# Hybrid pooling and SSD layer on one core: work of the mixing stage moved between VectorE and GpSimd, with other buffers and another order of loads at its start

## The chip, the cores and the metric

The kernel runs on one NeuronCore of one Trainium2 chip. The metric is the device time of one execution in microseconds (us), the median of the runs made; a lower time is better. In the views, PE is TensorE, PEld its weight loads, DVE is VectorE, ACT is ScalarE, POOL is GpSimd and SP is the engine whose queue issues nearly all DMAs.

## The reference, cut to what matters

One decoder layer works on 1024 prompt tokens and on 8 samples of 8 tokens each. Two gated feed-forward blocks enclose the token mixing, and the mixing is where the change lies:

```python
proj = hn @ w_in                       # u, z, x/B/C, dt, two gates
branch_pool = pool_mix(u) @ pool_w_out
xbc = silu(causal_conv(xbc))           # x: 32 heads of 64; B, C: 4 groups of 128
# SSD over chunks of 128 tokens, per head:
a_cs = cumsum(dt * A)                  # within the chunk
y    = ((C @ B.T) * exp(a_cs[l] - a_cs[s])) @ (dt * x)   # inside the chunk, causal
y   += exp(a_cs) * (C @ h_prev)                          # from the state
st   = B.T @ (exp(a_cs[-1] - a_cs) * dt * x)             # the chunk's state
h    = exp(a_cs[-1]) * h_prev + st
y    = y + d_skip * x
yg   = y * silu(z); yg = yg * rsqrt(mean(yg**2 over the group) + eps) * ssd_norm
merged = sigmoid(gate0) * branch_pool + sigmoid(gate1) * (yg @ ssd_w_out)
x = x + merged @ w_o
```

## The kernel before, in words

The tokens are worked on in two halves: half 0 has 512 prompt tokens, half 1 the other 512 and the 64 sample tokens (576 columns). Channels lie on the 128 partitions. Every f32 product of the large matrices is made of three fp32r products: ACT rounds an operand to a high part (L355 for activations, L294 for weights), DVE subtracts to get the low part (L357 or L359, L295), and PE adds three matmuls into one PSUM bank.

The program opens three stages, each with a pool of SBUF memory of its own: first feed-forward block and input projection, mixing, and second feed-forward block. A pool's memory is given to the next stage's tiles, so the first write into such a tile waits until the tile that lay there has been read for the last time. Two sets of buffers lie outside the stages: `act` (42 tiles) and `pair` (8 tiles). In the first stage `fx` takes from the stage's own pool (17 tiles).

In mixing, PE's main thread runs `pool_branch` for both halves (matmuls `pgm`, then `pbp`), then for each half `ssd_out` and `merge` (`pso`) and `out_proj` (`pwo`). Beside it runs the chain `scan`, which goes through eight groups of heads, (half, group) from (0,0) to (1,3). Chains are generators: the main thread calls `tick()` between blocks of matmuls, and a chain is continued when the estimated PE time that it asked for has gone by. The framework then orders each engine's queue by priority and an estimate of its own. Each engine works its queue strictly in order.

For a group, `fetch` loads B, C (`bc`) and x (`xs`, four blocks of channels). `ssd_a` for a chunk of 128 tokens loads `ab`, the cumulated a of the group's eight heads, to all partitions; PE turns x (`pxT`) and makes C·B (`pcb`); DVE makes `xdt` (x·dt, L1338) and `xd` (x·dt·decay, L1347), both from PSUM; ACT makes `ea` (L1355) and the decays (L1357, L1358), DVE multiplies them by the masked C·B (L1359); GpSimd scales x by d_skip (L1349). `ssd_st` makes the state with one matmul group `pst`, which needs `xd`. `ssd_b` makes `pyo` (from the state) and `pyd` (from `ab` and `xdt`), and adds them. In half 1 a fifth chunk has the samples: eight units, each of which loads a state `h`, scales and updates it (L1403) and stores it (L1405). `z` is loaded with chunk 3 of every group (L1470).

When a group is through, `gating` starts as a chain: y·z (L1495), the norm by `rstd` (squares on ACT, sums `ssq` on DVE L380, one matmul group `pss`, then `prb`), y·norm on DVE (L1504), and the split into `yhl` for the `pso` matmuls. `merge` combines the branches: a side chain `head` makes (1+gate)·acc on DVE (L1594) and adds the pooling branch on GpSimd (L1595) ahead of the last `pso` of each block; behind it two DVE steps (L1608, L1609) and the split into `mh`, `ml` remain.

Of the kernel before, what the change touches and what calls it, by code (L numbers as in the profile page):

```python
# [44 lines left out]
STEP_S = 1.0  # L45
POST, RIPE = 1.0, 3.0
GP = (1.5, 1.2)
# [14 lines left out]
def tile_hybrid_pool_ssd_macaron(  # L62
# [189 lines left out]
    acs_d = [dp.tile([4, NH, CH], F32, tag=f"acsd{h}", name=f"acsd{h}") for h in HALVES]  # L252
# [116 lines left out]
    def rstd(tiles, h, count, out, pace=1.0):  # L369

        N = NTOK[h]
        nch = 4 + h
        s = act((P, N), name="ssq")
        for i, x in enumerate(tiles):
            if i == 0:
                S.activation(s, x, AF.Square)
            else:
                q = act((P, N), name="sq")
                S.activation(q, x, AF.Square)
                V.tensor_tensor(s, s, q, op=ALU.add)  # L380
# [20 lines left out]
        S.copy(r[:, :512], pr)  # L401
# [425 lines left out]
    def mix_dt(h, xs):  # L827
# [9 lines left out]
        def chain():  # L837
# [43 lines left out]
            dma(acs_d[h].rearrange("c h l -> (c h) l"), afm)  # L881
            V.tensor_tensor(dtd, dtd, dt[:, :128], op=ALU.mult)
# [172 lines left out]
    def proj_pair(kind, ia, ib, xs):  # L1055
# [22 lines left out]
        def after(p, i, bk):  # L1078
# [3 lines left out]
            if p == "1":  # L1082
                out[i] = {"a": fx(name="ra"), "b": fx(name="rb")}
# [216 lines left out]
    def ssd_a(h, g, c, Bf, Cf, xs4, dts, h0s):  # L1300
# [11 lines left out]
        for q in range(nq):  # L1312
            ab = act((P, hq, L), name="ab")
            if smp:
                dma(ab, acs_sd[g * HPG : (g + 1) * HPG].partition_broadcast(P))
            else:
                r0 = g * HPG + q * hq
                dma(ab, acs_d[h][c, r0 : r0 + hq].partition_broadcast(P))
# [26 lines left out]
        else:  # L1345
            xd = act((P, 512), name="xd")
            V.tensor_tensor(xd[:L, :].rearrange("p (h d) -> p h d", d=HD), px[:L, :].rearrange("p (h d) -> p h d", d=HD),  # L1347
# [3 lines left out]
        for q, ab in enumerate(abs_):  # L1351
            av = ab.rearrange("p (q h) l -> p q h l", h=2)
            ev = ea[:, q * (hq // 2) : (q + 1) * (hq // 2), :]
            for hh in range(2):
                S.activation(ev[hh * HD : (hh + 1) * HD], av[hh * HD : (hh + 1) * HD, :, hh, :], AF.Exp)  # L1355
            for i in range(hq):
                S.activation(ab[:L, i, :], ab[:L, i, :], AF.Relu, bias=acs[:L, hc + q * hq + i : hc + q * hq + i + 1], scale=-1.0)  # L1357
            S.activation(ab[:L], ab[:L], AF.Exp, scale=-1.0)  # L1358
            V.tensor_tensor(ab[:L], ab[:L], cbm[:L, :L].unsqueeze(1).broadcast_to([L, hq, L]), op=ALU.mult)  # L1359
# [10 lines left out]
    def ssd_b(h, g, c, a, hold, Cf, y4, dts, h0s):  # L1370
# [8 lines left out]
        if smp:  # L1379
# [12 lines left out]
            for i, (pr, bh) in enumerate(units):  # L1392
# [12 lines left out]
                dma(dst, h0)  # L1405
                if pr == 3:
# [19 lines left out]
        for i in range(HPG):  # L1426
            m_ = abs_[i // abs_[0].shape[1]][:L, i % abs_[0].shape[1], :]
# [31 lines left out]

    def ssd_group(h, g, Bf, Cf, xs4, dts, zs):  # L1460
# [3 lines left out]
        for c in range(4 + h):  # L1464
            ga = ssd_a(h, g, c, Bf, Cf, xs4, dts, h0s)
            next(ga)
            if c == 3:
                for j in range(4):
                    z = act((P, NTOK[h]), name="z")
                    dma(z, zd[h][g * 4 + j])  # L1470
                    zs.append(z)
# [5 lines left out]
            if prev:  # L1477
                yield from ssd_b(h, g, *prev, Cf, y4, dts, h0s)
            prev = (c, a)
        yield step  # L1480
        yield from ssd_b(h, g, *prev, ssd_st(h, g, *prev, dts), Cf, y4, dts, h0s)
# [9 lines left out]
    def gating(h, g, y4, zs, out):  # L1491

        N = NTOK[h]
        for j in range(4):
            (G if j % 2 and (h, g) != (1, NG - 1) else V).tensor_tensor(y4[:, j, :N], y4[:, j, :N], zs[j], op=ALU.mult)  # L1495
            yield GP[0]
        rr = []
        yield from rstd([y4[:, j, :N] for j in range(4)], h, 512, rr, GP[0])
# [3 lines left out]
        for j in range(4):  # L1502
            a, b, _ = pair(N, "yhl")
            V.tensor_tensor(y4[:, j, :N], y4[:, j, :N], rr[0], op=ALU.mult)  # L1504
# [50 lines left out]
    cs = start(scan())  # L1555

# [25 lines left out]
    def merge(h, gs, acc):  # L1582
# [4 lines left out]

        def head():
# [9 lines left out]
        ch = start(head(), MP)  # L1598
        yn = ynorm(h, gs)
        mh, ml = [], []  # L1600
        for m in range(KD):
            pb = dense(ssd_w_out[0], gs[0] * 4, 4 * len(gs), m * P, [yn], name="pso")[0]
            while merged[0] <= m:
                ch.step()
            a_, b_ = act((P, N), F32R, "mh"), act((P, N), F32R, "ml")
            with tc.high_priority(HP_EV):
                for pt, (a, b) in zip(pb, PIECES[h]):
                    V.scalar_tensor_tensor(t1[m][:, a:b], t1[m][:, a:b], 1.0, pt[:, : b - a], op0=ALU.add, op1=ALU.mult)  # L1608
            V.tensor_tensor(t1[m], t1[m], acc[m], op=ALU.add)  # L1609
# [168 lines left out]
```

## Time and profile before

| | |
|---|---|
| median of 3 runs | 2937.12 us (2936.72 to 2939.24) |
| the profiled execution's own time | 2939.05 us |
| its span, first to last instruction | 2937.3 us |
| PE busy | 2828.8 us, 96% of the span |
| DVE, ACT, POOL busy | 1784.7, 1385.2 and 993.0 us |
| mixing stage | from about 1523 us (first `pgm`) to 2177 us (end of `pwo`) |

The profiled execution's time is its span and 1.75 us around it; it lies 1.93 us above the median. PE is busy nearly all the time, so a change can bring only what PE waits, what it runs at less than its full clock, and what it loses between instructions. These waits stand mostly between 1520 and 2060 us.

### The profile page before, as it was taken

What the parts mean: (1) busy time and instruction counts of PE and PEld (TensorE: products, weight loads), DVE (VectorE), ACT (ScalarE), POOL (GpSimd) and SP (SyncE); (2) the same over time, 40 slices, a digit from 0 to 9 for tenths busy, and PEclk for the clock granted to TensorE, in tenths of its full rate; (3) what the DMA queues carried; (4) which work ended last, traced back from release to release, by engine and by line L of the source; (5) the groups of instructions that cost most, each with busy time, mean ns of one, the idle gap of its engine ahead of it and who ended that gap; (6) DMA issues with size and microseconds to landing.
All of it is one profiled execution on the core that took longest, in us unless ns stands there. A gap on an engine that the chain in (4) does not pass through costs nothing.

```text
span 2937.3 us, 51029 instructions
## 1 busy us (share of the span) xinstructions
PE 2828.8 (96%) x18494; PEld 2570.2 (88%) x18494; DVE 1784.7 (61%) x2843; ACT 1385.2 (47%) x3024; POOL 993.0 (34%) x1011
## 2 busy tenths in 40 slices
PE   7999999999999999999989999898999999999998
PEld 6999999789989989898977887677999999987898
DVE  6655555434484687887976877766665544453422
ACT  5444444323354555564556766566233444442422
POOL 6434444000133455454422332323234444440000
PEclk9999999999999999999999999999999999999999
DMA  4575554856445555543367777786774532236652
GB/s 134 166 224 182 160 172 132 277 188 194 112 126 163 159 179 159 183 127 124 98 221 240 235 235 232 229 271 184 237 241 153 161 98 77 81 101 212 218 156 72
DMA packets 530332, 507.97 MB, mean 173 GB/s; under 512 B 36884, under 2 KB 374664, under 8 KB 530072
## 3 DMA queue, kind: packets, MB, share of 16 engines
q1 hardware_dynamic: 530064, 504.72, 54.0%
q8 instruction: 145, 2.38, 0.3%
q14 instruction: 107, 0.88, 0.1%
q10 hardware_dynamic: 16, 0.00, 0.0%
HBM read 361.77 MB, written 143.05 MB: 172 GB/s over the span
## 4 chain that ended last, share of the span: by engine, by line
PE 44%; DVE 6%; ACT 3%; DMA 3%; issue 1%; POOL 1%; SPq 1%; POOLq 0%; ACTq 0%; DVEq 0%
PE pw L163 19%; PE po L163 9%; PE pso L163 4%; PE pwo L163 3%; PE pbp L163 3%; PE pg L163 1%; PE pu L163 1%; ACT ab L1357 1%; PE pyd L163 1%; DVE wl L444 1%; DVE ct L940 1%; PE pst L163 1%; DMA wraw<-in_ffn_w_in_dram 0%; DVE xs L1504 0%; DVE ab L1359 0%
## 5 line engine op out<-in xcount | busy, mean ns | idle before, releaser
L163 PE MATMUL pw<-X,wh 128*128 128x288 f32 (+1 forms) x2484 | 624.0, 330 | 11.9 <-ACT t L1120 5.3
L163 PE MATMUL pw<-X,wl 128*128 128x288 f32 (+1 forms) x1644 | 472.9, 288 | 0.8 <-DVE wl L444 0.8
L163 PEld LDWEIGHTS pw<-X,wh 128*128 128x128 f32 x2484 | 417.7, 188 | 51.5 <-ACT t L1120 6.7
L163 PE MATMUL pw<-hl,wh 128*128 128x512 f32 x1072 | 390.5, 398 | 3.1 <-DVE t L1129 2.1
L444 DVE TENSOR_TENSOR wl<-s,wh 128x512 fp32r<-128x512 f32 x288 | 223.3, 776 | 200.6 <-ACT wh L443 179.1
L163 PE MATMUL pw<-hi,wh 128*128 128x288 f32 x1120 | 332.1, 297 | 1.3 <-ACT t L596 1.3
L163 PE MATMUL pw<-lo,wh 128*128 128x288 f32 x1120 | 329.7, 294 | 0.0
L163 PE MATMUL pw<-hi,wl 128*128 128x288 f32 x1120 | 329.6, 294 | 0.0
L295 DVE TENSOR_TENSOR wl<-wraw,wh 128x512 fp32r<-128x512 f32 x228 | 164.2, 721 | 249.2 <-ACT wh L294 236.9
L163 PEld LDWEIGHTS pw<-X,wl 128*128 128x128 f32 x1644 | 310.6, 189 | 1.9 <-DVE wl L444 1.8
L437 POOL TENSOR_TENSOR s<-wraw,wraw 128x512 f32<-128x512 f32 x144 | 196.0, 1361 | 333.7 <-DVE wl L444 216.7
L163 PE MATMUL pw<-hl,wl 128*128 128x256 f32 x1072 | 299.6, 280 | 0.2 <-DVE wl L444 0.2
L294 ACT ACTIVATE wh<-wraw 128x512 fp32r<-128x512 f32 x228 | 137.8, 606 | 326.0 <-PE po L163 229.1
L444 DVE TENSOR_TENSOR wl<-wraw,wh 128x512 fp32r<-128x512 f32 x216 | 177.0, 819 | 123.0 <-ACT wh L443 116.3
L443 ACT ACTIVATE wh<-s 128x512 fp32r<-128x512 f32 x288 | 180.8, 629 | 146.4 <-PE pw L163 139.1
L163 PEld LDWEIGHTS pw<-hl,wh 128*128 128x128 f32 x1072 | 201.9, 188 | 40.6 <-DVE t L1129 2.9
L163 PEld LDWEIGHTS pw<-hi,wh 128*128 128x128 f32 x1120 | 210.1, 188 | 12.6 <-ACT t L596 1.8
L163 PE MATMUL po<-hh,wh 128*128 128x288 f32 (+1 forms) x800 | 211.0, 324 | 3.6 <-ACT hh L355 3.4
L163 PE MATMUL po<-hh,wl 128*128 128x288 f32 (+1 forms) x800 | 210.9, 322 | 0.5 <-DMA wl<-part 0.5
L163 PE MATMUL po<-hr,wh 128*128 128x288 f32 (+1 forms) x800 | 210.9, 323 | 0.0
L163 PEld LDWEIGHTS pw<-lo,wh 128*128 128x128 f32 x1120 | 210.2, 188 | 0.0
L163 PEld LDWEIGHTS pw<-hi,wl 128*128 128x128 f32 x1120 | 210.1, 188 | 0.0
(384 smaller groups left out, 6340.7 us busy)
## 6 DMA issues: line engine op xcount, KB each, us to landing
wraw<-in_ffn_w_in_dram SPq DMA_DIRECT2D x188, 256.0 KB
wh<-part SPq DMA_DIRECT2D x156, 256.0 KB
wl<-part SPq DMA_DIRECT2D x156, 256.0 KB
wraw<-in_w_in_dram SPq DMA_DIRECT2D x144, 256.0 KB
wraw<-in_ffn_w_out_dram SPq DMA_DIRECT2D x120, 256.0 KB
part<-ph SPq DMA_DIRECT2D x80, 256.0 KB
part<-pr SPq DMA_DIRECT2D x80, 256.0 KB
ab<-acsd SPq DMA_DIRECT2D x64, 256.0 KB
```

What stands on the lines that cost most here:

```text
L163: T.matmul(out, lhsT, rhs, start=start, stop=stop, skip_group_check=free)
L294: S.activation(wh, raw, AF.Copy)
L295: V.tensor_tensor(wl, raw, wh.bitcast(F32), op=ALU.subtract)
L437: G.tensor_tensor(t, a, b, op=op)
L443: S.activation(wh, a, AF.Copy)
L444: V.tensor_tensor(wl, a, wh.bitcast(F32), op=ALU.subtract)
L940: V.scalar_tensor_tensor(o, f(j), w[j], o, op0=ALU.mult, op1=ALU.add)
L1357: S.activation(ab[:L, i, :], ab[:L, i, :], AF.Relu, bias=acs[:L, hc + q * hq + i : hc + q * hq + i + 1], scale=-1.0)
```

## The change

It has six parts, all in mixing or at its start.

1. `xd` is made by GpSimd from `xdt` (in SBUF) instead of by DVE from PSUM; for that the decay `dtd` is no longer multiplied by dt beforehand.
2. `gating` multiplies y by the norm factor on GpSimd, except for the last group (1,3), pauses 1.5 of estimated PE time behind each such step, and `rstd` waits 2.5 longer there before its matmuls `pss` are queued.
3. `merge` of half 0 works in another order: acc + pso first, then (1+gate) times it, both on DVE, and the pooling branch is added last, by GpSimd. There is no `head` chain; the loads run two blocks ahead.
4. Heads of a group are held as even and odd ones: `ab`'s first tile has heads 0, 2, 4, 6, its second 1, 3, 5, 7. Each tile takes one ACT step for `ea` instead of two of half the length. The table `acs_d` in DRAM is written in that order, by eight DMAs per half instead of one; the samples' `ab` comes by two DMAs of 256-byte rows instead of one of 2 KB rows.
5. In half 1 `z` is loaded within the samples' units (after unit 4's state is stored), not with chunk 3.
6. The last gate blocks of the input projection take `ra` and `rb` from `act`, not from the stage's pool, and `scan` is started one step ahead, so that its first loads are recorded ahead of `pool_branch`.

```diff
-        yield 2.0 * max(pace, 0.75)
+        yield wait + 2.0 * max(pace, 0.75)
...
-            dma(acs_d[h].rearrange("c h l -> (c h) l"), afm)
-            V.tensor_tensor(dtd, dtd, dt[:, :128], op=ALU.mult)
+            for i in range(HPG):
+                dma(acs_d[h][:, :, i % 2, i // 2, :].rearrange("c g l -> (c g) l"), afm[i::HPG])
...
-                out[i] = {"a": fx(name="ra"), "b": fx(name="rb")}
+                new = act if len(xs) == 1 else fx
+                out[i] = {"a": new(name="ra"), "b": new(name="rb")}
...
-            V.tensor_tensor(xd[:L, :]..., px[:L, :]..., dtd..., op=ALU.mult)
+            G.tensor_tensor(xd[:L, :]..., xp[:L, :]..., dtd..., op=ALU.mult)
...
+                if i == Z_UNIT:
+                    load_z(h, g, zs)
...
-            if c == 3:
+            if c == 3 and h == 0:
...
-            V.tensor_tensor(y4[:, j, :N], y4[:, j, :N], rr[0], op=ALU.mult)
+            (V if last else G).tensor_tensor(y4[:, j, :N], y4[:, j, :N], rr[0], op=ALU.mult)
+            if not last:
+                yield GP[0]
...
     cs = start(scan())
+    cs.step()
...
+                    if h == 0:
+                        V.tensor_tensor(acc[m][:, a:b], acc[m][:, a:b], pt[:, : b - a], op=ALU.add)
...
+            if h == 0:
+                V.scalar_tensor_tensor(t1[m], t1[m], 1.0, acc[m], op0=ALU.add, op1=ALU.mult)
+                G.tensor_tensor(t1[m], t1[m], acs[m], op=ALU.add)
+            else:
+                V.tensor_tensor(t1[m], t1[m], acc[m], op=ALU.add)
```

Three places show how the queues change. The first is SP's queue where mixing begins: `gd` is the store of the last gate blocks, `dts`, `bc` and `xs` are the first loads of `scan`, `wraw` are weights. Before:

```order
L916 DMA gd_4_220<-ra_17602 128x576
L291 DMA wraw_18055<-in_pool_w_out_dram 128x4x128
L916 DMA gd_5_221<-rb_17603 128x576
L1318 DMA ab_17773<-acsd_115 128x512
L1318 DMA ab_17775<-acsd_115 128x512
L291 DMA wraw_18073<-in_pool_w_out_dram 128x4x128
L1526 DMA dts_17753<-dtp_272 128x576
L1518 DMA bc_17755<-cv_16_136 128x512
L1519 DMA bc_17756<-cv_20_140 128x512
L1521 DMA xs_3234_17757<-cv_0_120 128x512
```

And in the changed kernel:

```order
L291 DMA wraw_17931<-in_pool_w_out_dram 128x4x128
L1534 DMA dts_17748<-dtp_272 128x576
L1526 DMA bc_17750<-cv_16_136 128x512
L1527 DMA bc_17751<-cv_20_140 128x512
L1529 DMA xs_3228_17752<-cv_0_120 128x512
L1529 DMA xs_3228_17752<-cv_1_121 128x512
L1529 DMA xs_3228_17752<-cv_2_122 128x512
L916 DMA gd_4_220<-ra_17614 128x576
L1529 DMA xs_3228_17752<-cv_3_123 128x512
L1526 DMA bc_17759<-cv_17_137 128x512
L916 DMA gd_5_221<-rb_17615 128x576
```

`dts` and the x of the first group now stand ahead of the two gate stores, not behind them, and five loads of `pool_w_out` weights that stood ahead of `dts` follow later. In the built program `dts` waits for the two `gd` stores before the change, and for the four `zd` stores (which stand ahead of both pieces) after it.

The second is PE's queue where the norm of group (0,3) is made (`pss` needs `ssq`, the sum of squares). Before:

```order
L163 MATMUL pso_20505<-yhl_19401,wh_20506 128x512 x2
L163 MATMUL pso_20505<-yhl_19401,wl_20508 128x512
L163 MATMUL pso_20505<-yhl_19430,wh_20506 128x512
L163 MATMUL pss_20496<-ones,ssq_20398 128x1 x4
L163 MATMUL pso_20505<-yhl_19430,wh_20506 128x512
L163 MATMUL pso_20505<-yhl_19430,wl_20508 128x512
L163 MATMUL pyo_20516<-bc_19684,hst_20361 128x128 x4
L163 MATMUL pyd_20521<-ab_20323,xdt_20376 64x128 x4
L163 MATMUL pyd_20521<-ab_20325,xdt_20376 64x128 x4
```

And in the changed kernel, from the same block of `pso` on:

```order
L163 MATMUL pso_20471<-yhl_19563,wh_20472 128x512 x2
L163 MATMUL pso_20471<-yhl_19563,wl_20474 128x512
L163 MATMUL pyo_20485<-bc_19672,hst_20337 128x128 x4
L163 MATMUL pyd_20490<-ab_20293,xdt_20352 64x128
L163 MATMUL pyd_20490<-ab_20295,xdt_20352 64x128
L163 MATMUL pyd_20490<-ab_20293,xdt_20352 64x128
L163 MATMUL pyd_20490<-ab_20295,xdt_20352 64x128
L163 MATMUL pyd_20490<-ab_20293,xdt_20352 64x128
L163 MATMUL pyd_20490<-ab_20295,xdt_20352 64x128
L163 MATMUL pyd_20490<-ab_20293,xdt_20352 64x128
L163 MATMUL pyd_20490<-ab_20295,xdt_20352 64x128
L163 MATMUL pss_20506<-ones,ssq_20372 128x1 x4
```

`pss` moved behind the rest of that block, `pyo` and `pyd`; `pyd` now takes its two `ab` tiles in turn.

The third is GpSimd's queue in the merge of half 0: `acc` or `t` with `ac` is the addition of the pooling branch, `xs` with `r` the norm factor, `xd` the state's scaled x, `hst` the old state's decay, `xs` with `ea` the sum of y. Before, around the fifth to seventh addition:

```order
L1454 TENSOR_TENSOR hst_21417<-hst_21288,dts_18337 128x512
L1595 TENSOR_TENSOR acc_3736_20089<-acc_3736_20089,ac_21402 128x512
L1437 TENSOR_TENSOR xs_3770_20240<-xs_3770_20240,ea_21308 128x4x128
L1595 TENSOR_TENSOR acc_3749_20147<-acc_3749_20147,ac_21457 128x512
L1349 TENSOR_TENSOR xs_3770_20240<-xs_3770_20240,Dcol 128x4x64
L1595 TENSOR_TENSOR acc_3753_20166<-acc_3753_20166,ac_21494 128x512
```

And in the changed kernel, from the fourth addition to the seventh:

```order
L1635 TENSOR_TENSOR t_3990_21238<-t_3990_21238,ac_21239 128x512
L1456 TENSOR_TENSOR hst_21364<-hst_21255,dts_18323 128x512
L1510 TENSOR_TENSOR xs_3656_19673<-xs_3656_19673,r_21347 128x576
L1348 TENSOR_TENSOR xd_21381<-xdt_21379,dts_18323 128x512
L1510 TENSOR_TENSOR xs_3656_19673<-xs_3656_19673,r_21347 128x576 x2
L1635 TENSOR_TENSOR t_4008_21314<-t_4008_21314,ac_21315 128x512
L1510 TENSOR_TENSOR xs_3656_19673<-xs_3656_19673,r_21347 128x576
L1439 TENSOR_TENSOR xs_3770_20218<-xs_3770_20218,ea_21275 128x4x128
L1350 TENSOR_TENSOR xs_3770_20218<-xs_3770_20218,Dcol 128x4x64
L1635 TENSOR_TENSOR t_4031_21411<-t_4031_21411,ac_21412 128x512
L1456 TENSOR_TENSOR hst_21489<-hst_21364,dts_18323 128x512
L1439 TENSOR_TENSOR xs_3770_20218<-xs_3770_20218,ea_21384 128x4x128
```

The four norm factors of group (1,0) and an `xd` now stand between the additions, and the additions themselves lie behind the last DVE step of each block.

More of the change, by code (lines that the diff above doesn't have):

```diff
@@ L367, in along, with rstd @@
         tr(out, r[:n, i : i + 1].broadcast_to([n, P]), ident[:n, :n])
-    def rstd(tiles, h, count, out, pace=1.0):
+    def rstd(tiles, h, count, out, pace=1.0, wait=0.0):
         N = NTOK[h]
@@ L1458, in ssd_st, with load_z @@
         return hold
+    def load_z(h, g, zs):
+        for j in range(4):
+            z = act((P, NTOK[h]), name="z")
+            dma(z, zd[h][g * 4 + j])
+            zs.append(z)
     def ssd_group(h, g, Bf, Cf, xs4, dts, zs):
@@ L1466, in ssd_group @@
             next(ga)
-            if c == 3:
[L1468 to L1471, printed above, removed]
+            if c == 3 and h == 0:
+                load_z(h, g, zs)
             yield step
@@ L1493, in gating @@
         N = NTOK[h]
+        last = (h, g) == (1, NG - 1)
         for j in range(4):
[L1495 removed]
+            (G if j % 2 and not last else V).tensor_tensor(y4[:, j, :N], y4[:, j, :N], zs[j], op=ALU.mult)
             yield GP[0]
         rr = []
[L1498 removed]
+        yield from rstd([y4[:, j, :N] for j in range(4)], h, 512, rr, GP[0], G_WAIT)
         while h * NG + g - 2 >= freed[0]:
@@ L1586, in merge, with load @@
         merged = [0]
+        acs = [None] * KD
+        def load(m):
+            if h == 0 and m < KD:
+                t1[m], acs[m] = act((P, N), name="t1"), act((P, N), name="ac")
+                dma(t1[m], gd[h][KD + m])
+                dma(acs[m], accd[h][m])
         def head():
@@ L1596, in head @@
                 merged[0] += 1
-        ch = start(head(), MP)
+        if h == 1:
+            ch = start(head(), MP)
+        for m in range(2):
+            load(m)
         yn = ynorm(h, gs)
```

46 lines of the change are left out of this document (23 added, 23 removed).

## The prediction, made before the changed kernel ran

> **What bounds the kernel now.** I read the page first, then stretches of the mixing stage, then what PE waited for there, then the chain at the worst place.
>
> The page's busy times, and the stretches with the lowest PE share (columns: length, busy time and instructions of PE, PEld, DVE, ACT, POOL, granted PE clock, DMA share and rate; the last row sums ten stretches that cover 1520 to 2060 us):
>
> ```profile
> PE 2828.8 (96%) x18494; PEld 2570.2 (88%) x18494; DVE 1784.7 (61%) x2843; ACT 1385.2 (47%) x3024; POOL 993.0 (34%) x1011
> ...
> 1520.00:1550.00 30.00, 20.33 (x80) 15.53 (x80) 13.31 (x21) 17.09 (x33) 1.04 (x1) 0.77 0.82 260
> 1760.00:1780.00 20.00, 17.79 (x107) 14.02 (x105) 14.63 (x23) 13.81 (x37) 8.34 (x9) 0.91 0.59 188
> 1836.00:1880.00 44.00, 35.53 (x174) 26.67 (x175) 37.58 (x52) 18.02 (x45) 19.99 (x16) 0.88 0.64 212
> 1980.00:2010.00 30.00, 21.88 (x132) 17.77 (x131) 17.28 (x28) 17.60 (x47) 13.35 (x10) 0.77 0.63 197
> sum 540.00, PE 498.02 PEld 408.46 DVE 378.67 ACT 344.05 POOL 163.11; mean PE 49.80 PEld 40.85 DVE 37.87 ACT 34.41 POOL 16.31
> ```
>
> PE is the bound and its matmuls stay, so only waits and a low clock can be won. From 1520 to 2060 us PE stands idle for 540.0 - 498.0 = 42 us, and it runs below its clock in four short stretches, each of them one with a long wait. DVE has 379 of 540 us and is next to full in the merge (37.6 of 44); GpSimd has 163.
>
> What PE waited for in those 540 us (us in total, times, longest):
>
> ```profile
> PE pst L163 <- DVE xd L1347: 6.5, 4, 4.0
> PE pss L163 <- DVE ssq L380: 5.9, 3, 2.7
> PE pxT L167 <- DMA xs<-cv: 4.4, 3, 3.6
> PE pgm L163 <- DMA d<-dh: 4.3, 1, 4.3
> PE pso L163 <- ACT acc L1577: 3.2, 1, 3.2
> PE pwo L163 <- DVE t L1608: 3.1, 1, 3.1
> PE pgm L163 <- DVE fl L359: 2.9, 3, 1.2
> ```
>
> Two causes: loads at the start of mixing (4.4 + 4.3 = 8.7), and DVE's results (6.5 + 5.9 + 3.1 + 2.9 = 18.4).
>
> **Part by part. The start of mixing.** The chain there (start, length, what), with the stores and the first loads:
>
> ```profile
> 1513.30 0.32 SPq L921 DMA_DIRECT2D zd<-rb  x1
> ...
> 1523.92 5.32 DMA gd<-rb
> 1529.31 0.32 SPq L1526
> 1531.57 5.14 DMA xs<-cv
> 1536.77 5.68 DMA d<-dh
> ...
> 1531.12 0.39 PE L163 MATMUL pgm<-d,wl 128*128 128x512 f32 x1
> 1535.16 0.44 PE L167 MATMUL pxT<-ident,xs 128*128 128x128 f32 x1 [3.65 <-DMA xs<-cv]
> 1542.59 1.39 PE L163 MATMUL pgm<-d,wh 128*128 128x512 f32 x2 [4.34 <-DMA d<-dh]
> ```
>
> The first load of `scan` goes into memory of `ra` and `rb`, so it waits until the store of `rb` has landed: 1523.92 + 5.32 = 1529.24, and it is issued at 1529.31. Behind it on SP stand x, and behind x the operands `d` of the last `pgm`: both PE waits hang on this one store. With `ra` and `rb` in `act` the load waits for the store of `zd` issued at 1513.30; by the same 5.32 that is 1518.6, 10.7 us earlier. `dts`, `bc` and `xs` then go out from 1518.6 on, the fourth `xs` behind the first gate store, at about 1523; landed by the same 5.14 at 1528. PE's order now has `pxT` behind four of the eight `pgm`, which by the present pace (six between 1523.0 and 1531.5) are through at about 1528.5, so the wait of 3.65 goes. What is late next is `d`: it stands on SP behind `ab` and five weight loads. It goes out at about 1530 instead of 1536.8, and as transfers are dense here (share 0.82), I put its landing at 1536 to 1537, where PE arrives at 1535 to 1536, having done a `pst` and another `pxT` early. Idle time in the stretch is 30.00 - 20.33 = 9.7 us, and the clock of 0.77 costs (1 - 0.77) x 20.33 = 4.7 more. I take 8.0 of these 14.4, not less than 3 (the first wait alone, less a little), not more than 11.
>
> **Steps taken from DVE.** The groups between 1520 and 2060 us (busy us, mean ns | idle before):
>
> ```profile
> L1359 DVE TENSOR_TENSOR ab<-ab,cbm 128x512 f32<-128x512 f32 x64 | 54.2, 849 | 31.0 <-ACT ab L1358 30.9
> L1347 DVE TENSOR_TENSOR xd<-pxT,dts 128x512 f32<-128x512 f32 x32 | 21.7, 677 | 0.0
> L1504 DVE TENSOR_TENSOR xs<-xs,r 128x512 f32<-128x512 f32 x16 | 13.0, 836 | 1.0 <-ACT r L401 1.0
> L1504 DVE TENSOR_TENSOR xs<-xs,r 128x576 f32<-128x576 f32 x12 | 11.6, 983 | 0.0
> L1609 DVE TENSOR_TENSOR t<-t,acc 128x512 f32<-128x512 f32 x8 | 8.5, 1068 | 1.6 <-POOL acc L1595 1.4
> L1454 POOL TENSOR_TENSOR hst<-hst,dts 128x512 f32<-128x512 f32 x28 | 34.3, 1226 | 1.7 <-ACT hst L1452 0.9 <-issue 0.9
> L1437 POOL TENSOR_TENSOR xs<-xs,ea 128x512 f32<-128x512 f32 x28 | 41.7, 1491 | 144.4 <-DVE ea L1436 120.1 <-ACT yhl L355 6.2 <-ACT ea L1355 4.8
> L1495 POOL TENSOR_TENSOR xs<-xs,z 128x576 f32<-128x576 f32 x6 | 10.7, 1786 | 0.2
> L1595 POOL TENSOR_TENSOR acc<-acc,ac 128x512 f32<-128x512 f32 x8 | 11.3, 1411 | 20.2 <-DVE acc L1594 16.1 <-DMA ab<-acsd 4.2
> ```
>
> `xd` (21.7), the norm factor (13.0 + 11.6) and one step per block of the merge (8.5) leave DVE: 54.8 of 379 us. On GpSimd `xd` is shaped as the step on `hst` (32 x 1.23 = 39), the norm factor as those on `ea` and z (16 x 1.49 + 12 x 1.79 = 45): 84 more on 163, 46% of 540 us.
>
> Two forms of DVE steps behave differently beside GpSimd (min/median/max ns):
>
> ```profile
> L1359 DVE TENSOR_TENSOR ab<-ab,cbm x68: 676/692/1819, 1541.9 to 2034.2; 128x512 f32<-128x512 f32 x64, 64x512 f32<-64x512 f32 x4
> L1347 DVE TENSOR_TENSOR xd<-pxT,dts x32: 672/677/683, 1538.9 to 2019.8; 128x512 f32<-128x512 f32 x32
> ```
>
> A step with an input in PSUM is never stretched; one with both inputs in SBUF takes 676 alone and 849 in the mean. That mean excess of 173 ns stands at 163 us of GpSimd; at 247 it would be 173 x 247 / 163 = 262, 89 more. Over the 64 steps on `ab` and, as an estimate, about as many again on weights and splits, 12 us come back to DVE, which keeps a net relief of some 43 us, a ninth of its work. The Trainium skill, "SBUF — State Buffer", section "Who interferes with whom", says that a VectorE instruction with two SBUF inputs and a GpSimd instruction that reads SBUF lock each other out for the whole instruction, and that one with at most one SBUF input does not contend. The trace agrees in kind (1819 against 683 at most); taken at its full price the rule speaks against this change, and that is the third rival.
>
> What that is worth where PE waits: `pss` of group (0,3) now stands behind eight `pso`, `pyo` and `pyd`, about 4 us of PE work, so its wait of some 2 us goes; the longest `pst` wait,
>
> ```profile
> 1987.14 1.10 PE L163 MATMUL pst<-xd,btok 128*128 128x512 f32 x2 [4.01 <-DVE xd L1347]
> ```
>
> gets 26 `pso` matmuls in front of it in PE's order, some 3.5 us. So of 18.4 us I take 3.5 of `pss`, 4.5 of `pst`, 1.0 of `pwo`, 1.5 of `fl`: 10.5, not less than 5 and not more than 18. With shorter waits the clock falls less: outside the start it cost 0.09 x 17.8 + 0.12 x 35.5 + 0.23 x 21.9 = 10.9 us, of which I take 4.0 (0 to 9).
>
> **What GpSimd gives back.** `xd` now ends 1.23 us behind `xdt` instead of 0.68, and it queues: behind it stand the d_skip step, `hst` and the sum of y. In the merge four norm factors (1.79 each), three `xd` (1.23) and two more additions (1.41) join 20 us in a stretch of 44: 34 us, with the last addition now ahead of the split that `pwo` needs. I take +5.0 for `pst` and `pwo` waiting on GpSimd (0 to 20).
>
> **The rest.** ACT's `ea` goes from two half-length steps to one; the trace has the half length at 411 ns and an ACT step of full length at 618:
>
> ```profile
> L1355 ACT ACTIVATE ea<-ab 64x256 f32<-64x256 f32 x136 | 55.9, 411 | 15.0 <-DMA ab<-acsd 13.4
> L1358 ACT ACTIVATE ab<-ab 128x512 f32<-128x512 f32 x64 | 39.5, 618 | 0.1
> ```
>
> That is 128 x 0.411 - 64 x 0.618 = 13 us of ACT, off the path but for the one wait on ACT (3.2). Against it, `pyd` needs both `ab` tiles at its second matmul; before, four matmuls later. Loading z late puts four loads behind a store that waits for DVE (first row: issue of unit 4's store or one next to it; second: a z load's flight; third: the first use):
>
> ```profile
> 1975.78 0.39 SPq L1405 DMA_DIRECT2D out_dram<-h  x1
> 1630.03 5.28 DMA z<-zd
> 1983.17 0.76 DVE L1495 TENSOR_TENSOR xs<-xs,z 128x576 f32<-128x576 f32 x1 [0.93 <-POOL xs L1437]
> ```
>
> 7.4 us for four issues and a flight of 5.3: just in time, or 1 us late, four times. The 14 extra stores of `acs_d` and the four extra loads of the samples' `ab` have six weight buffers as cover and cost nothing; without it, under half a microsecond of SP each, 7 us. I take +2.0 together (-3 to +9).
>
> Sum: -8.0 - 10.5 - 4.0 + 5.0 + 2.0 = -15.5. From the profiled execution's 2939.05 that is 2923.6; it lies 1.93 above the median, so 2921.6, or **2921.5**.
>
> **The rivals.** *All that PE waits on DVE and loads goes* and GpSimd keeps up: -11 - 18 - 9 + 2 = -36, 2901. For: GpSimd is a third busy. Against: the merge. *Only the start pays*, because DVE's lag comes from what DVE waits for (31 us on `ab` from ACT alone) and not from its work: -8 + 2, 2931. *The lock takes it all back:* every step moved to GpSimd holds up a DVE step with two SBUF inputs for its whole length; 60 steps of 1.23 to 1.79 us are 84 us against 54.8 removed, so DVE's waits grow by half of 18.4 where the start gives 8: +9 - 8 = +1, 2938. The row of 849 against 676 speaks for a sixth of that. *GpSimd becomes the late one* (slower): PE reaches `pst` just as `xd` ends in 4 of 32 chunks (the four waits above). If `xdt` comes no earlier, `xd` comes 0.55 later plus one queued GpSimd step of 1.49, 2.0 us; with the chunks next in line say eight times, 16 us, in the merge another 6, and the clock falls again at half of these places, 1.5 us each, 6: +28 - 8 = +20 with nothing won, 2957; it ends slower than before once it costs more than about 14 us. For it: 34 of 44 us in the merge, strictly in order. Against it: half 0, where PE leaves several us between `xd` and `pst` and the trace shows no wait. *The start does not gain*, if loads there are bound by transfer rate: 2929.5; I count it with the second.
>
> **How the numbers follow.** A measurement tells 0.2%, 5.9 us, from no change. Forecast 0.50 (2912 to 2930); all waits 0.10; only the start 0.12, of which half ends within 5.9 us of before; lock 0.11, mostly within it; GpSimd late 0.17. Faster: 0.50 + 0.10 + 0.06 + 0.01 = 0.67; same: 0.06 + 0.08 = 0.14; slower 0.17 + 0.02 = 0.19. For the range I leave out most of the first rival and the upper half of the last: 2906 to 2945.
>
> **What would show it.** Right: no wait of PE on `xs` or `d` above 2 us at the start, `dts` issued before 1520 us; no wait of `pss` on `ssq` above 1 us; a PE clock of 0.95 or more between 1980 and 2010; DVE 35 to 50 us less and GpSimd 75 to 95 us more in mixing. Wrong: `pst` or `pwo` waiting on POOL for more than 10 us together, means of the steps on `ab` above 1000 ns, or z as a releaser.

## The result, and the profile after

The changed kernel ran 2940.74 us (median; 2936.95 to 2944.00, 12 runs) beside 2938.68 us for the kernel before (2934.87 to 2942.66, 12 runs): a ratio of 1.0007, interval 0.9998 to 1.0015. That is no change within 0.2%, 19 us above the forecast of 2921.5.

The page's busy times of the changed kernel, and stretches of its mixing stage (columns as in the prediction; the fifth row is the whole of 1520 to 2060 us):

```profile
PE 2831.6 (96%) x18494; PEld 2573.3 (88%) x18494; DVE 1749.5 (60%) x2777; ACT 1373.8 (47%) x2964; POOL 1072.9 (37%) x1071
```

```profile
1520.00:1550.00 30.00, 24.48 (x121) 19.53 (x120) 14.18 (x24) 18.18 (x36) 3.58 (x3) 0.94 0.94 286
1760.00:1780.00 20.00, 18.78 (x122) 14.79 (x120) 16.72 (x25) 13.28 (x32) 13.03 (x12) 1.00 0.58 199
1836.00:1880.00 44.00, 38.21 (x211) 29.13 (x211) 34.84 (x49) 24.14 (x61) 31.73 (x24) 0.93 0.71 230
1980.00:2010.00 30.00, 25.55 (x186) 22.56 (x184) 16.04 (x26) 15.86 (x40) 16.08 (x13) 0.90 0.76 247
1520.00:2060.00 540.00, 500.54 (x3362) 412.08 (x3361) 345.82 (x522) 333.66 (x835) 240.38 (x189) 0.97 0.75 236
```

The work moved as forecast: DVE is 35.2 us lower, GpSimd 79.9 us higher. All four stretches with a low clock are better than before (0.94, 1.00, 0.93, 0.90 against 0.77, 0.91, 0.88, 0.77). But PE's idle time in the 540 us is 540.0 - 500.5 = 39.5 us, against 42.0: DVE lost 33 us of work there, and PE got back 2.5. The waits of PE show what came instead:

```profile
PE pgm L163 <- DVE fl L359: 8.3, 3, 3.6
PE pst L163 <- POOL xd L1348: 6.3, 3, 3.3
PE pb L167 <- DVE hst L1458: 4.0, 2, 3.2
PE pss L163 <- DVE ssq L380: 3.7, 2, 1.9
...
PE pgm L163 <- DMA d<-dh: 1.7, 1, 1.7
```

The waits on x are gone, that of `pwo` on `t` (3.1) too, and that on `d` is 1.7 against 4.3. But `fl` (the low part of pool_branch's activations) holds PE for 8.3 against 2.9 (2.3 of it at the start of mixing, 6.0 in half 1's `pgm`), `pst` waits for `xd` almost as long as before, on the other engine, and `pb` behind `hst` is new. Behind PE's waits stand those of DVE and ACT on GpSimd:

```profile
DVE hst L1458 <- POOL hst L1456: 15.5, 8, 5.9
```

```profile
ACT yhl L355 <- POOL xs L1510: 18.3, 10, 9.0
```

The first of these was 0.8 us before; but no_gp below, which leaves both steps on DVE, has 5.8, so not all of it comes from the moves. The second stood on DVE before: ACT's splits waited 13.6 us for the norm factor there, 4.7 less. The start itself went as argued; SP's queue in the changed kernel:

```profile
1516.47 0.32 SPq L921 DMA_DIRECT2D zd<-rb  x1
1522.10 0.32 SPq L1534 DMA_DIRECT2D dts<-dtp  x1
```

`dts` is issued 5.63 us behind the last `zd` store (the forecast had 5.32), and 4.6 us ahead of the first `pgm` (1526.70); before, it came 6.3 us behind the first `pgm`.

### The profile page after: what moved, and what is told of

Its sections match the earlier page's. It is cut to its first block, busy times and chain, and to the rows that moved or that the text cites. A ratio compares the mean times of both kernels' runs of the same rounds, so it can differ in the third digit from the quotient of the medians.

```text
span 2939.0 us, 51028 instructions
## 1 busy us (share of the span) xinstructions
PE 2831.6 (96%) x18494; PEld 2573.3 (88%) x18494; DVE 1749.5 (60%) x2777; ACT 1373.8 (47%) x2964; POOL 1072.9 (37%) x1071
```

## The experiments

Each kernel takes some of the six parts of the change, numbered as above. All were timed beside the kernel before, whose median in these sets was 2938.2 to 2940.1, so medians of different sets compare to about 2 us. The last column is one profiled execution, from the start of the first `pgm` to that of the last `pwo`; before has 652.8 there, the changed kernel 649.3. It doesn't always follow the median: the profiled execution was the shortest of all runs for no_xd (2932.88), seam_merge (2927.97) and norm_nowait (2930.61), and 4 us above the median for xd_twice (2932.34).

| kernel | what it has | us, median | ratio to before (95%) | mixing, us |
|---|---|---|---|---|
| seam_only | 6 (start) | 2932.21 | 0.9974 (0.9964 to 0.9983) | 645.5 |
| seam_merge | 6 and 3 (merge) | 2932.54 | 0.9983 (0.9974 to 0.9991) | 641.4 |
| seam_heads | 6 and 4 (heads) | 2932.79 | 0.9974 (0.9964 to 0.9985) | 647.7 |
| seam_z | 6 and 5 (z) | 2934.89 | 0.9983 (0.9973 to 0.9992) | 647.1 |
| heads_only | 4 | 2938.17 | 0.9998 (0.9989 to 1.0007) | 652.0 |
| wait_only | the pause of part 2 | 2946.49 | 1.0029 (1.0018 to 1.0041) | 658.8 |
| no_gp_nowait | 3, 4, 5, 6 | 2927.26 | 0.9961 (0.9949 to 0.9974) | 640.4 |
| best (the same again) | 3, 4, 5, 6 | 2925.75 | 0.9960 (0.9944 to 0.9975) | 637.1 |
| xd_twice | 3 to 6, idle copy of xd on GpSimd | 2928.32 | 0.9970 (0.9960 to 0.9980) | 644.1 |
| xd_nowait | 3 to 6 and 1 (xd) | 2936.57 | 0.9989 (0.9981 to 0.9998) | 647.4 |
| norm_nowait | 3 to 6, norm factor on GpSimd and the short pauses behind its steps | 2933.58 | 0.9987 (0.9978 to 0.9995) | 641.2 |
| no_wait | all but the pause | 2943.03 | 1.0011 (1.0002 to 1.0019) | 657.7 |
| no_gp | 3 to 6 and the pause | 2939.38 | 1.0000 (0.9991 to 1.0009) | 647.1 |
| pause_00 | 3 to 6, pause in group (0,0) | 2930.58 | 0.9971 (0.9959 to 0.9983) | 643.1 |
| pause_rest | 3 to 6, pause in the others | 2931.77 | 0.9972 (0.9960 to 0.9984) | 641.9 |
| no_norm | all but the norm factor's move and its short pauses | 2937.08 | 0.9994 (0.9986 to 1.0003) | 650.7 |
| no_xd | all but xd's move | 2940.50 | 1.0002 (0.9993 to 1.0012) | 647.2 |
| all_pause_rest | all, no pause in (0,0) | 2937.13 | 0.9996 (0.9986 to 1.0006) | 650.1 |

**First set: is it GpSimd?** Theory A: the start gains, and GpSimd's longer queue gives it back. Rival B: the gain is lost within pool_branch whatever GpSimd does. Rival C: the loss lies ahead of mixing. seam_only has this diff against before, and nothing else that changes what runs:

```diff
-                out[i] = {"a": fx(name="ra"), "b": fx(name="rb")}
+                new = act if len(xs) == 1 else fx
+                out[i] = {"a": new(name="ra"), "b": new(name="rb")}
...
     cs = start(scan())
+    cs.step()
```

> The kernel before with part 6 alone (ra and rb of the last gate blocks from act, scan started one step ahead). Theory A (the start gains what its trace shows, and GpSimd's longer queue gives it back later): 6 us faster than before, 4 to 8, with dts issued some 11 us earlier against the first pgm. Theory B (the start's gain is lost again within pool_branch whatever GpSimd does, since the next waits there are on DVE or on transfers): within 2 us of before, though the first pbp comes 4 us earlier. Theory C (the changed kernel loses ahead of mixing): as A here.

The next three undo moves of the changed kernel: no_gp both pieces, no_norm the second, no_xd the first (and with `xd` back on DVE, `dtd` is multiplied by dt again). The second piece also takes away the short pause behind each step.

```diff
-            G.tensor_tensor(xd[:L, :]..., xp[:L, :]..., dtd..., op=ALU.mult)
+            V.tensor_tensor(xd[:L, :]..., px[:L, :]..., dtd..., op=ALU.mult)
...
-            (V if last else G).tensor_tensor(y4[:, j, :N], y4[:, j, :N], rr[0], op=ALU.mult)
-            if not last:
-                yield GP[0]
+            V.tensor_tensor(y4[:, j, :N], y4[:, j, :N], rr[0], op=ALU.mult)
```

> The changed kernel with xd (from PSUM, dtd times dt) and the norm factor back on DVE; merge order, heads, z, start and the longer wait ahead of pss stay. Theory A: 8 to 14 us faster than before: the waits of DVE on the hst step, of PE on xd and of ACT on the norm factor (15.5, 6.3 and 18.3 us in the changed kernel) are gone, and the start's gain stays. Theory B: within 3 us of before. Theory C (the loss lies ahead of mixing, in the eight stores of acs_d): still 2 us slower than seam_only.

> The changed kernel with the norm factor alone back on DVE; xd stays on GpSimd. Theory A, norm factor as the culprit: 6 to 10 us faster than before, the waits of DVE on hst fall from 15.5 to under 5 us. Theory A, xd as the culprit: within 2 us of before, and the hst waits stay above 10 us. Theory B: within 3 us of before.

> The changed kernel with xd alone back on DVE; the norm factor stays on GpSimd. Theory A, xd as the culprit: 5 to 9 us faster than before, no wait of PE on GpSimd at pst. Theory A, norm factor as the culprit: within 3 us of before, ACT still waiting 15 us or more on the norm factor. Theory B: within 3 us of before.

seam_only gains 7 us, so the start's term holds (8.0 forecast) and B falls. Its waits at the start, from 1515 to 1550 us, have 0.8 us on `d` where before had 4.3, and 2.3 on `fl`, which are new there:

```profile
PE pgm L163 <- DVE fl L359: 2.3, 1, 2.3
...
PE pgm L163 <- DMA d<-dh: 0.8, 1, 0.8
```

But no_gp, with DVE doing everything as before, is not faster than the changed kernel by more than its interval (2939.38), and no_norm and no_xd also stay within 3 us of before. Theory A as it stood fell: something besides the moves takes the start's gain, and the traces put it into half 1's `pgm`. Measured from the first `pgm`, the last one starts at 107.0 us in seam_only and at 112.7 in no_gp and in the changed kernel. C fell too: from the first matmul of the first block's second matrix (`po`) to the first `pgm` it takes 997.1 us in before, 997.8 in the changed kernel and 997.3 in no_gp.

**Second set: which part takes it?** The candidates were the pause (P), the heads (Q), and merge or z (R). The edit of wait_only against before comes down to one argument (`G_WAIT` is 2.5), and no_wait sets it to 0 in the whole change; no_gp_nowait is no_gp with 0:

```diff
-        yield from rstd([y4[:, j, :N] for j in range(4)], h, 512, rr, GP[0])
+        yield from rstd([y4[:, j, :N] for j in range(4)], h, 512, rr, GP[0], G_WAIT)
```

> The kernel before with one thing from the change: the longer pause of 2.5 ahead of pss in gating. P, the pause moves the norm factors and splits of group (0,0) into half 1's pgm, where PE needs fl at once, and takes back the start's gain: 2943 to 2945 (4 to 6 above before), with fl waits of PE after 1610 us of 3 us or more in one piece. Q, the even and odd heads do it (pyd waits for both ab tiles): 2939. R, it is the merge or z: 2939.

> The whole change but the longer pause. P (the pause takes the start's gain and GpSimd is neutral): 2932 to 2935. Q (the heads): 2938 to 2941. R (merge or z): 2938 to 2941. If both this and the kernel without the GpSimd moves and pause come out at 2932, the GpSimd moves bring nothing; if this one is 3 us or more below it, they bring what was forecast in part.

> The changed kernel with xd and the norm factor on VectorE and without the longer pause: what is left is the start's buffers, the merge's order, the heads and z. P (the pause): the start's gain comes back, 2931 to 2934, the end of pgm at 107 to 108 us after the first one. Q (the heads): 2938 to 2940, pgm ends at 112 us or later. R (merge or z): 2938 to 2940, with pgm's end at 107 and the loss after pwo begins or in the samples' units.

heads_only holds a group's heads as even and odd, and writes the table so:

```diff
-            dma(acs_d[h].rearrange("c h l -> (c h) l"), afm)
+            for i in range(HPG):
+                dma(acs_d[h][:, :, i % 2, i // 2, :].rearrange("c g l -> (c g) l"), afm[i::HPG])
```

> The kernel before with only the heads held as even and odd (one ACT step per tile for ea, eight stores of acs_d per half). P (the pause): 2938 to 2939.5, as before. Q (the heads): 2943 to 2945, with pyd waiting on ab by 4 us more in the trace. R (merge or z): 2938 to 2939.5.

The pause costs 7 us alone and 12 on top of parts 3 to 6 (2927.26 to 2939.38); the heads cost nothing. In wait_only the loss doesn't lie where P had it: the last `pgm` starts 113.7 us after the first, against 114.4 in before, and the one long wait on `fl` (3.5 us) is that of the first `pbp` behind it. And no_wait came out at 2943.03, 8 us above the top of what P gave it: without the pause, the GpSimd moves cost 16 us (2927.26 to 2943.03). So there are two losses that don't add, not one (with pause and moves together the kernel is at 2940.74). PE's waits from 1515 to 2070 us without the moves (no_gp_nowait), then with them (no_wait):

```profile
PE pst L163 <- DVE xd L1349: 5.4, 3, 4.0
...
PE pss L163 <- DVE ssq L380: 4.4, 3, 1.9
```

```profile
PE pst L163 <- POOL xd L1348: 11.2, 5, 4.8
PE pss L163 <- DVE ssq L380: 8.1, 3, 3.4
```

And the whole of 1520 to 2060 us in the same order:

```profile
1520.00:2060.00 540.00, 508.08 (x3443) 420.07 (x3442) 376.47 (x589) 338.10 (x842) 168.84 (x130) 0.98 0.75 239
```

```profile
1520.00:2060.00 540.00, 497.26 (x3315) 407.54 (x3313) 344.10 (x516) 331.32 (x830) 237.21 (x189) 0.96 0.73 233
```

DVE is relieved of 32 us, and PE is idle for 42.7 us instead of 31.9, at a lower clock.

**Third set: late results, or a loaded GpSimd?** L: a moved result is ready later and PE waits for that. K: GpSimd's added time itself holds up everything that it and DVE do in SBUF. xd_nowait and norm_nowait are no_gp_nowait with one move each (first and second piece of the diff above, the other way). xd_twice tells L from K: DVE makes `xd` and its result is used, and GpSimd makes it a second time:

```diff
+    spare = stage["p"].tile([P, 512], F32, tag="spare", bufs=1, name="spare")
...
             V.tensor_tensor(xd[:L, :]..., px[:L, :]..., dtd..., op=ALU.mult)
+            G.tensor_tensor(spare[:L, :]..., xp[:L, :]..., dtd..., op=ALU.mult)
```

> The changed kernel without the longer pause and with the norm factor on VectorE, so that only xd is moved to GpSimd on top of the start, the merge, the heads and z (which alone ran 2927.3). Both moves together without the pause ran 2943.0, 15.8 more. L, each moved result is ready later and PE waits for it: about 2936 (the pst waits on xd were 5.8 us longer with both moved, plus the clock behind them). K, GpSimd's added time holds up everything that it and VectorE do in SBUF, in proportion to 36 of 77 us: about 2935, with all of VectorE's two-SBUF-input steps longer. If it is 2928 or less, xd on GpSimd is free and the norm factor costs it all.

> The changed kernel without the longer pause and with xd on VectorE, so that only the norm factor (and the short pauses behind its steps) is moved to GpSimd on top of the 2927.3 kernel. L: about 2933, since the norm factor is needed only by pso, later, and costs mainly through xs and yhl waits of ScalarE. K: in proportion to 41 of 77 us, about 2935. If it is 2940 or more, the norm factor is what costs.

> The 2927.3 kernel (start, merge, heads, z; no pause; xd and norm factor on VectorE) with 32 added GpSimd steps that make xd a second time into a spare tile that nobody reads. PE's order is the same. L (lateness of the moved result): 2927 to 2930, since VectorE's xd is used and comes as early as before. K (lock and queue on GpSimd): 2934 to 2940, with hst on GpSimd later, VectorE's steps on ab at 930 ns or more against 833, and pst or pyd waiting for hst.

L holds for `xd`: against the two medians of the kernel without moves (no_gp_nowait and best), its move costs 9 to 11 us and the copy 1 to 3, with as many steps added to GpSimd and none taken from DVE. PE's waits from 1515 to 2070 us and the 540 us in xd_nowait,

```profile
PE pst L163 <- POOL xd L1348: 10.4, 4, 6.0
PE pss L163 <- DVE ssq L380: 8.1, 3, 3.4
```

```profile
1520.00:2060.00 540.00, 499.44 (x3388) 413.26 (x3389) 362.19 (x550) 335.91 (x837) 200.81 (x161) 0.97 0.75 236
```

and the same in xd_twice:

```profile
PE pss L163 <- DVE ssq L380: 5.7, 3, 2.3
PE pst L163 <- DVE xd L1350: 5.3, 3, 4.0
```

```profile
1520.00:2060.00 540.00, 506.05 (x3413) 417.66 (x3411) 381.98 (x585) 337.66 (x841) 204.40 (x161) 0.97 0.75 238
```

The move of `xd` alone brings most of what `pst` and all of what `pss` gained in no_wait; the copy leaves `pst` where it was (5.4). PE is idle for 40.6 us with the move, 34.0 with the copy, and 31.9 and 30.4 in no_gp_nowait and best.

The norm factor's move costs 6 to 8 us. But it has no copy of its own to tell L from K, and its edit holds the short pauses behind each step as well, which no run separates: that its cost is lateness is not shown.

What the load of the copy does to DVE: the groups in xd_twice, then the one of `ab` in no_gp_nowait (best, the same kernel, has 844 ns):

```profile
L1363 DVE TENSOR_TENSOR ab<-ab,cbm 128x512 f32<-128x512 f32 x64 | 54.4, 851 | 26.5 <-ACT ab L1362 26.3
```

```profile
L1352 POOL TENSOR_TENSOR spare<-xdt,dts 128x512 f32<-128x512 f32 x32 | 35.6, 1114 | 35.8 <-DVE xdt L1341 34.1 <-DMA xs<-cv 1.5
```

```profile
L1360 DVE TENSOR_TENSOR ab<-ab,cbm 128x512 f32<-128x512 f32 x64 | 53.2, 833 | 28.2 <-ACT ab L1359 28.2
```

35.6 us of added GpSimd steps stretch the steps on `ab` by 7 to 18 ns each. DVE's busy time in the 540 us is 382.0 against 376.5 and 379.8, 2 to 6 us more, and over the whole program 1788.7 against 1779.6 and 1782.2, 7 to 9 more. The two profiles of one kernel lie 3 us apart themselves, so this is a rough size: about a quarter of the 35.6 at most. What lateness looks like at the longest `pst` wait: GpSimd in xd_nowait, DVE with the step that feeds it, and PE; then the same place in best, where DVE makes `xd`:

```profile
1973.14 1.97 POOL L1501 TENSOR_TENSOR xs<-xs,z 128x576 f32<-128x576 f32 x1
1975.07 1.55 POOL L1350 TENSOR_TENSOR xs<-xs,Dcol 128x512 f32<-128x512 f32 x1
1976.58 1.39 POOL L1501 TENSOR_TENSOR xs<-xs,z 128x576 f32<-128x576 f32 x1
1977.94 1.04 POOL L1348 TENSOR_TENSOR xd<-xdt,dts 128x512 f32<-128x512 f32 x1
```

```profile
1973.09 0.76 DVE L1501 TENSOR_TENSOR xs<-xs,z 128x576 f32<-128x576 f32 x1 [0.93 <-POOL xs L1439]
...
1973.97 1.75 DVE L1501 TENSOR_TENSOR xs<-xs,z 128x576 f32<-128x576 f32 x1
1975.65 0.68 DVE L1339 TENSOR_TENSOR xdt<-pxT,dts 128x512 f32<-128x512 f32 x1
1979.67 0.69 DVE L1661 TENSOR_TENSOR x<-x,pwo 128x512 f32<-128x512 f32 x1 [3.35 <-DMA x<-xspill]
```

```profile
1979.03 2.08 PE L163 MATMUL pst<-xd,btok 128*128 128x512 f32 x2 [5.98 <-POOL xd L1348]
```

```profile
1969.17 0.68 DVE L1340 TENSOR_TENSOR xdt<-pxT,dts 128x512 f32<-128x512 f32 x1
1969.78 0.67 DVE L1349 TENSOR_TENSOR xd<-pxT,dts 128x512 f32<-128x512 f32 x1
```

```profile
1970.60 2.05 PE L163 MATMUL pst<-xd,btok 128*128 128x512 f32 x2 [4.01 <-DVE xd L1349]
```

On DVE, `xd` ends 1.28 us after `xdt` begins; on GpSimd 3.33 us, since it stands behind the end of the d_skip step (`Dcol`) and a z step. PE's wait grows from 4.01 to 5.98 us, and one near 1907 us from 1.09 to 3.28. Both stand at the first chunk of a group of half 1, behind the y·z steps of the group before, on either engine. What made PE wait in the first place are the two z steps on DVE ahead of `xdt`, 2.5 us, and the move doesn't touch them; DVE then has 3.35 us with nothing to do.

For the norm factor PE is not the one that waits first. Its result goes to ACT's split, and GpSimd's old steps queue behind it. ACT in no_gp_nowait, then ACT and DVE in norm_nowait:

```profile
ACT yhl L355 <- DVE xs L1511: 16.9, 8, 8.9
```

```profile
ACT yhl L355 <- POOL xs L1511: 20.5, 12, 8.0
```

```profile
DVE hst L1459 <- POOL hst L1457: 12.3, 8, 3.8
```

ACT's wait for the norm factor is 4 us longer than on DVE, and that on `hst` 6 us (6.5 in no_gp_nowait). How the 6 to 8 us come out of this stays open: PE's waits for `pst` and `pss` are 11.4 us together, hardly more than the 9.8 and 10.1 without the move, and the profiled execution, the shortest of the kernel's runs, has hardly a longer mixing stage (641.2).

**What parts 3, 4 and 5 bring beside the start.** seam_only's edit and one part more each; seam_merge has the other order of the merge in half 0,

```diff
+                    if h == 0:
+                        V.tensor_tensor(acc[m][:, a:b], acc[m][:, a:b], pt[:, : b - a], op=ALU.add)
```

> The kernel before with the start's buffers and the merge's other order only. If the merge's order is what separates the 2927.3 kernel from the start alone (2932.2): 2926 to 2929. If heads or z do it: 2931 to 2934.

seam_heads has the edit of heads_only, and seam_z loads z within the units in half 1:

```diff
+                if i == Z_UNIT:
+                    load_z(h, g, zs)
...
-            if c == 3:
+            if c == 3 and h == 0:
```

> The kernel before with the start's buffers and the even and odd heads only. If the heads bring the 5 us between start and merge (2932.5) and the kernel with heads and z too (2926.5): 2926 to 2929. If z does: 2931 to 2933.

> The kernel before with the start's buffers and z within the samples' units only. If z brings the 5 us: 2926 to 2929, with fewer transfers ahead of the merge's loads. If the heads do: 2931 to 2933.

None of the three gains over the start alone (2932.2); all three together are 5 to 6 us better (2927.3 and 2925.8). That they bring it only together is what the medians say, but the intervals of the single ones reach down to 0.9964 and those of the sum up to 0.9975, so it is not settled.

**Fourth set: where does the pause cost?** P0: only in group (0,0), whose gating it pushes into half 1's `pgm`. P1: in every group.

pause_00 has this diff against no_gp; pause_rest (against no_gp) and all_pause_rest (against the changed kernel) have the two values the other way round:

```diff
-        yield from rstd(..., h, 512, rr, GP[0], G_WAIT)
+        yield from rstd(..., h, 512, rr, GP[0], G_WAIT if (h, g) == (0, 0) else 0.0)
```

> The 2927.3 kernel (start, merge, heads, z; xd and norm factor on VectorE) with the longer pause for group (0,0) alone. P0, the pause costs because the first group's norm factors and splits fall between half 1's fl: 2936 to 2940, as with the pause for all groups (2939.4), with one fl wait of PE of 3 to 4 us in half 1's pgm. P1, the pause costs a little in every group: 2929 to 2931.

> The 2927.3 kernel with the longer pause for all groups but (0,0). P0: 2925 to 2929. P1: 2934 to 2938.

> The whole change, with the longer pause for all groups but (0,0). P0: the whole change had the last pgm 2.7 us later than without the pause but then gained it back and more by the end of pwo; so without the first pause 2932 to 2936 (2940.7 less 5 to 8). P1: 2940 to 2943.

> The kernel with start, merge, heads and z and without the two GpSimd moves and the pause, once more: 2926 to 2930 if its first measurement (2927.3, 5 runs) holds.

P0 fell, and of P1's sizes only that of pause_00 held: the first group's pause costs 3 to 5 us, the others' 4.5 to 6 (both intervals still touch that of best), and all of them 12 to 14. With the pause, the two moves cost only 1 us more (2939.38 to 2940.74) instead of 16, and neither of them alone changes the time measurably (no_xd 2940.50, no_norm 2937.08): the losses overlap. The waits show where: all those of `pst` and `pss` together, whoever ended them, are 9.8 us in no_gp_nowait and 23.0 in no_wait, but 10.6 in no_gp and 11.9 in the changed kernel. Without the pause the moves lengthen them by 13 us, with it by 1. Why the pause does this stays open. In all_pause_rest, taking the first group's pause away brings 3.6 us (the intervals overlap), less than P0 had. The first group's cost is seen in the trace. PE in pause_00, then in best:

```profile
1624.49 0.85 PE L163 MATMUL pgm<-d,wh 128*128 128x288 f32 x2 [4.05 <-DVE fl L359]
```

```profile
1622.42 0.53 PE L163 MATMUL pgm<-d,wh 128*128 128x288 f32 x2 [1.61 <-DVE fl L359]
```

And what DVE does ahead of that `fl` in no_gp, which has the same wait (4.06 us, ended at 1626.69):

```profile
1621.13 0.69 DVE L1511 TENSOR_TENSOR xs<-xs,r 128x512 f32<-128x512 f32 x1
1621.74 1.76 DVE L1360 TENSOR_TENSOR ab<-ab,cbm 128x512 f32<-128x512 f32 x1
1623.42 1.52 DVE L1511 TENSOR_TENSOR xs<-xs,r 128x512 f32<-128x512 f32 x1
1624.86 0.74 DVE L359 SCALAR_TENSOR_TENSOR yhl<-xs,cols,yhl 128x512 fp32r<-128x512 f32 x1
1625.53 0.68 DVE L1511 TENSOR_TENSOR xs<-xs,r 128x512 f32<-128x512 f32 x1
1626.13 1.79 DVE L359 SCALAR_TENSOR_TENSOR fl<-pgm,cols,fh 128x288 fp32r<-128x288 f32 x4
```

Three norm factors and a split stand ahead of the `fl` that PE needs, 5.0 us of DVE in one run, with the step on `ab`. The delay lasts: the last `pgm` starts 112.5 us after the first in pause_00 and at 105.8 in best and pause_rest. Where the other groups' pause costs stays open: the longest wait in pause_rest is one of 3.6 us on `ssq` near 1992 us (1.7 in best), and its mixing stage is 1.5 to 4.8 us longer than the two profiles without it.

No kernel ran faster than best, which is 0.4% below before and 15 us below the changed kernel.

## Why the prediction was wrong

**The start (-8.0): right.** 7 us in seam_only, by the chain as told: the waits on x are gone and that on `d` is 0.8. In their place 2.3 us on `fl` are new, which the working did not have.

**Steps taken from DVE (-10.5) and GpSimd gives back (+5.0): this failed.** The sum of the two was -5.5 and -9.5 with the clock's term; the two moves cost +16 without the pause, and together with the pause, as the change has them, +14 (2926.5, the middle of the two medians without either, to 2940.74), of which the pause alone makes 12 to 14. The failing step is "what that is worth where PE waits": 18.4 us of PE's waits name DVE, and the working took that for a lack of DVE's time as a whole. Of its four gains, `pwo` came in full (3.1 us, 1.0 forecast) and `pss` for the most part (2.2 of 3.5); `pst` gained 0.2 of 4.5, since the longest wait fell from 4.0 to 2.6 but another grew from 1.3 to 3.3, and `fl` lost 5.4 where 1.5 were to be won. A step that leaves a queue helps only what stands behind it there. At the long `pst` wait PE waits for the moved step itself: what stands ahead of it on DVE (z, `xdt`) stays, and its new queue is slower and has steps in it. The relief was real (33 of a forecast 43 us, from 378.7 to 345.8), and PE's idle time grew by 10.8 us where only the moves were added.

**The rival "GpSimd becomes the late one"** had the mechanism, for `xd`, and its price at one place: 2.0 us later per `xd` where PE reaches `pst` first, and 2.05 us later was measured there. The total is about half of what it had: 28 us forecast, 16 measured for both moves without the pause, 9 to 11 of them for `xd`. It got a chance of 0.17, and what stood against it was half 0, where the trace before shows no wait. In no_wait half 0 does add little (two waits of 0.7 and 1.3 us); most of the cost lies in half 1, at two places that waited before, too. The working also put the d_skip step behind `xd` on GpSimd; in xd_nowait it stands directly ahead of `xd` in 19 of the 32 chunks.

**The pause: not priced.** It costs 12 to 14 us beside parts 3 to 6, and the sum has no term for it. It was counted only as what moves `pss` away from its wait. What is queued behind `pss` moves too: the norm factors and splits of the first group go to the place where PE needs `fl`. Of the 5.4 us that `fl` lost, 2.3 are those at the start; the other 3 are here, and pause_00 has them (7.6 on `fl` against 5.1 in best).

**The lock (rival 3): its price fell.** At full length it would have cost DVE 35.6 us in xd_twice; it was 2 to 9. The Trainium skill, "SBUF — State Buffer", section "Who interferes with whom", tells of the exclusive lock between the two; the trace agrees that steps with two SBUF inputs are stretched (ahead of the `fl` above, 1.76 us for one of 0.69, while a GpSimd step ran), but most are not: the median of the steps on `ab` in xd_twice is 689 ns. The forecast's scale (173 ns of excess at 163 us of GpSimd, in proportion) gives 38 ns more for those 36 us; 7 to 18 were measured.

**The clock (-4.0 outside the start):** by the granted clock in their rows, the three stretches lose 0.00 x 18.8 + 0.07 x 38.2 + 0.10 x 25.6 = 5.2 us against 10.9, but 1600 to 1640 us, at 1.00 before, now runs at 0.91:

```profile
1600.00:1640.00 40.00, 33.57 (x226) 29.19 (x225) 28.53 (x47) 23.78 (x55) 18.53 (x14) 0.91 0.75 237
```

That is 0.09 x 33.6 = 3.0 us, and 2.7 us of the 4.0 are left.

**Heads, z, stores (+2.0):** a gain of 5 to 6 us together with the merge, or nothing; no cost was found.

Of the signs that were named, the waits on `xs` and `d` and the totals of DVE and GpSimd came as forecast (DVE's 35.2 just within its 35 to 50). `dts` was issued at 1522.1 us, not before 1520, but mixing began 3.7 us later in this profile; against the first `pgm` it is 1518.4. The wait of `pst` on GpSimd stayed under 10 us (6.3) and the mean of the steps on `ab` under 1000 ns (885); the clock from 1980 to 2010 us (0.90) and `pss` (1.9 us at most) did not. The limit of 10 us for `pst` was no good sign: without the pause it is 11.2 us and the time is 2943.0, with it 6.3 us and 2940.7.

## What to carry to other kernels

Moving a step to another engine helps what stands behind it in the old queue and delays whoever waits for the step itself: look which of the two the bound engine is waiting for, and what stands in the new queue at that moment, before any shares of busy time. A copy of the moved step whose result nobody reads tells the load that it adds from the lateness of its result. A pause in one thread of work moves everything behind it: look at what the main thread needs at the new place, and price that, too.

## What the hardware showed that was not expected

Up to the second matrix of the first feed-forward block no kernel differs from another, and yet its first matmul (`po`) starts at 522.8 us in the profile of no_xd and at 529.9 in that of no_gp. With 7 us of that, the span of a single profile can't tell effects of this size. Times measured from the first `pgm` do better, though the same kernel's mixing stage still differs by 3.3 us (640.4 and 637.1); medians of many runs are the surest.

Two GpSimd steps of the same shape don't take the same time (no run shows why): 128x512 takes 1.1 us as `xd` from `xdt` (1114 ns in xd_twice), and 1.4 as the norm factor (1370 ns in norm_nowait):

```profile
L1511 POOL TENSOR_TENSOR xs<-xs,r 128x512 f32<-128x512 f32 x16 | 21.5, 1370 | 8.4 <-ACT r L401 8.4
```

The first was forecast at 1226 ns by the step on `hst`, the second at 1491 by that on `ea`; both were a little cheaper than taken, and still late.
